# A transformer layer's last product, cut by row blocks and with its weights split beforehand

## The chip, the cores and the metric

One core of one Trainium2 chip. The metric is the device time of one execution in microseconds; a time is the median of several executions. The engines are called PE (matmul), PEld (its weight load), DVE (vector), ACT (scalar activations), POOL (GpSimd) and SP (which issues transfers).

## The reference

One layer: a sliding-window attention mixer, then a gated embedding, then a final norm, for 512 positions of width 2048. The change touches only the last lines:

```python
y = swa_mixer(hn, swa_w_in[j], swa_w_out[j], swa_sinks[j], rel_bias)
x = x + y
emb = p[i] @ ple_proj[i]                                   # 512x256 @ 256x2048
g = jax.nn.sigmoid(rmsnorm(x, ple_norm[i]) @ ple_gate[i])  # 512x2048 @ 2048x2048
x = x + emb * g
...
return rmsnorm(x, final_g)
```

All is float32.

## The kernel before

**Split operands.** A float32 product is made of three matmuls in the fp32r type: each operand is split into a rounded high part and the rest, and `mm3` (L114 to L119) adds high x high (L117), low x high (L118) and high x low (L119). A split is a copy on ACT (`hi`) and a subtraction on DVE (`lo`); for weights it works on pieces of 128 x 1024.

**Seven products.** The product with `ple_gate` is done on half blocks with seven products instead of eight, in the order `ORDER_PLE = (2, 7, 1, 6, 5, 3, 4)`; the last is product 4. Each product `p` has two units `(p, jj)`, `jj` being a half of 512 columns. A unit takes four weight pieces; for each piece it does 12 matmuls of 512 columns into two PSUM banks (two row blocks `tb` of 128 rows). So a unit is 48 matmuls. Behind products 1, 5, 3 and 4 come the `e` matmuls (`embed`), 6 for a row block, with a piece of `ple_proj` (kind "proj").

**Pieces.** `B` (class `Pieces`) loads weight pieces and splits them in order, two pieces ahead of use, into the tags `whi` and `wlo` of three buffers each, so a split waits until PE is done with the piece three places before. Pieces of products 7, 6 and 4 "grow": one tile stays in SBUF and POOL issues a transfer that adds the next weights into it (`_prepare`, L537), once the piece of the product before is split. Of the last product's pieces, the last two are split in halves of 512 columns into the tags `ah` and `al` (L550 to L558).

**Gates.** `gate` takes a unit's banks, subtracts or adds kept partial sums, and `gated` does for one row block and 512 columns: a sigmoid on ACT (L876), times `e` and plus `x` on DVE (L877, L879), and the sum of squares for the final norm (ACT L881, or DVE L883 in the last row block's second column block). Rows 2 and 3 of the four row blocks, columns 0 and 1 of the four column blocks, come from product 4. `finish` makes a row block's norm from the sums (L895 to L904: the root on ACT, the rest on DVE), and `store` scales and writes it (L911 on DVE for rows 0 and 1; L915 and L917 on DVE and ACT for rows 2 and 3, which POOL has multiplied by `final_g` before, L887 and L984 to L986). Rows 2 and 3 issue half their stores from ACT's queue.

**Order.** PE and SP keep the order in which the program is written. In this stage the order of ACT, DVE and POOL is chosen by the framework's scheduler, which takes what is ready by its own reckoning; each engine then works through its queue in that order. In the program's text, `todo` and `later` spread the side work over a unit's four pieces.

**The last product before.** Unit (4,0) runs over both row blocks with its pieces from `B`. Then, for the second column half, row block 0 over 512 columns and row block 1 in two halves of 256 (L987 to L1004), tile `last`, each followed by `embed` and `gated`.

Of the kernel before, what the change touches and what calls it, by code (L numbers as in the profile page):

```python
# [39 lines left out]
PAD = 40  # L40
# [13 lines left out]
def trunk_kernel(ctx: ExitStack, tc: tile.TileContext, a: dict):  # L54
# [88 lines left out]

    def rsqrt_mean(out, ssq, n, nm):
# [12 lines left out]
        nc.vector.tensor_mul(out, y, t)  # L157
# [20 lines left out]
    for k in range(KC):  # L178
# [44 lines left out]
        if k == 9:  # L223
            rsqrt_mean(rstd1, ssq1, D, "r1")
# [298 lines left out]
    class Pieces:  # L523
# [22 lines left out]
        def _split(self, i):  # L546
            raw = self.base.pop(i)
            if i > len(self.specs) - 3:

                self.made[i] = [], []  # L550
                for k in range(2):
                    hi = acts.tile([P, 512], F32R, tag="ah", name=f"bhi{i}_{k}")
                    lo = acts.tile([P, 512], F32R, tag="al", name=f"blo{i}_{k}")
                    nc.scalar.copy(hi, raw[:, k * 512 : (k + 1) * 512])
                    nc.vector.tensor_sub(lo, raw[:, k * 512 : (k + 1) * 512], hi.bitcast(F32))
                    self.made[i][0].append(hi)
                    self.made[i][1].append(lo)
                return  # L558
            hi = wpool.tile([P, WE], F32R, tag="whi", name=f"bhi{i}")
            lo = wpool.tile([P, WE], F32R, tag="wlo", name=f"blo{i}")  # L560
            nc.scalar.copy(hi, raw)  # L561
            nc.vector.tensor_sub(lo, raw, hi.bitcast(F32))  # L562
            self.made[i] = tuple([t[:, :512], t[:, 512:]] for t in (hi, lo))
# [3 lines left out]
        def ahead(self, i):  # L567
            last = len(self.specs) - 1
# [22 lines left out]
    def add_stage(nm, order):  # L591
# [7 lines left out]
        for p in order:  # L599
            for jj in range(2):  # L600
                if (p, jj) == (4, 1):
                    add_embeds(p, jj)
# [9 lines left out]
                if (p, jj) != (4, 1):  # L612
# [134 lines left out]
    def run(gen):  # L747
        for _ in gen:
            pass

# [121 lines left out]
    def gated(t, j, zin, z, e_ps, c=slice(0, 512)):  # L872

        n = done[t]
        done[t] += 1
        nc.scalar.activation(z, zin, AF.Sigmoid, scale=rstd2[:, t : t + 1])  # L876
        nc.vector.tensor_mul(z, e_ps[:, c], z)  # L877
        xt = x1[j][:, t, c]
        nc.vector.tensor_add(xt, xt, z)  # L879
        if (t, j) != (3, 1):  # L880
# [5 lines left out]
        if (t, j) in ((2, 1), (3, 1)):  # L886
            nc.gpsimd.tensor_mul(xt, xt, fg[:, j * 512 + c.start : j * 512 + c.stop])  # L887

    def finish(t):

        n = done[t]
        base, ms, rt, y, nw, yn = (
            const.tile([P, 1], F32, name=f"{v}_{t}") for v in ("base", "ms", "rt", "y", "nw", "yn")
        )
        nc.vector.tensor_reduce(base, ssq3[:, t, : n - 1], axis=AX.X, op=ALU.add)  # L895
        nc.vector.tensor_scalar(base, base, 1.0 / D, EPS, op0=ALU.mult, op1=ALU.add)
        nc.vector.scalar_tensor_tensor(
            out=ms, in0=ssq3[:, t, n - 1 : n], scalar=1.0 / D, in1=base, op0=ALU.mult, op1=ALU.add
        )
        nc.scalar.activation(rt, ms, AF.Sqrt)  # L900
        nc.vector.reciprocal(y, rt)
        nc.vector.scalar_tensor_tensor(out=nw, in0=y, scalar=ms, in1=y, op0=ALU.mult, op1=ALU.mult)
        nc.vector.tensor_scalar(nw, nw, -0.5, 1.5, op0=ALU.mult, op1=ALU.add)
        nc.vector.tensor_mul(yn, y, nw)  # L904
        return [partial_of(store, t, j, yn) for j in range(4)]

    def store(t, j, yn):
        xt = x1[j][:, t, :]
        queue = nc.sync
        if t < 2:  # L910
            nc.vector.scalar_tensor_tensor(  # L911
                out=xt, in0=xt, scalar=yn, in1=fg[:, j * 512 : (j + 1) * 512], op0=ALU.mult, op1=ALU.mult
            )
        elif j < 2:
            nc.vector.tensor_scalar_mul(xt, xt, yn)  # L915
        else:
            nc.scalar.mul(xt, xt, yn)  # L917
            queue = nc.scalar
        queue.dma_start(a["out"][t * P : (t + 1) * P, j * 512 : (j + 1) * 512], xt)
# [4 lines left out]
    def gate(p, jj, ps, e):  # L924

        zs = []
        for tb in range(2):
# [13 lines left out]
            elif p == 3:  # L941
                zs.append((tb, 2 + jj, ps[tb], late.tile([P, 512], F32, tag="junk", name=f"z{jj}_{tb}", bufs=3)))
            else:
                nc.vector.tensor_sub(v2, ps[tb], v2)
                zs.append((2 + tb, jj, v2, v2))
        later[:0] = [partial_of(gated, *z, e[z[0]]) for z in zs]

    for n, p in enumerate(ORDER_PLE):
        nxt = ple_forms.steps(ORDER_PLE[n + 1]) if n < 6 else iter(())
        for jj in range(2):  # L950

            def todo():
                if turns:
                    turn(*turns.pop(0), "s")
                    if not turns:
                        nc.vector.tensor_reduce(ss2, ssq2, axis=AX.X, op=ALU.add)
                        rsqrt_mean(rstd2, ss2, D, "r2")
# [5 lines left out]
            if (p, jj) == (4, 1):  # L963
                break
            ps = unit(p, jj, at_ple, ple_forms, todo)
            e = {}
            if p in (1, 5, 3, 4):
# [3 lines left out]
            later.insert(0, partial_of(gate, p, jj, ps, e))  # L971
        run(nxt)
        if p == 3:
            for t in range(2):
                later.append(partial_of(lambda t: later.extend(finish(t)), t))


    f = ple_forms.made[4]
    first = at_ple[4, 1]
    w = B.get(first - 1)  # L980
    last = [B.get(first + m) for m in range(4)]
    for j in (2, 3):
        for t in (2, 3):
            later.append(partial_of(nc.gpsimd.tensor_mul, x1[j][:, t, :], x1[j][:, t, :], fg[:, j * 512 : (j + 1) * 512]))  # L984
    for t in (2, 3):
        later.append(partial_of(nc.gpsimd.tensor_mul, x1[0][:, t, :], x1[0][:, t, :], fg[:, :512]))  # L986
    for tb in range(2):  # L987
        cuts = [slice(0, 512)] if tb == 0 else [slice(0, 256), slice(256, 512)]
        for n, c in enumerate(cuts):
            ps = bank(f"last{tb}_{n}", "ps"[n])  # L990
            for k in range(8):
                fh, fl = f[k // 2]
                bh, bl = last[k // 2]
                mm3(ps[:, c], fh[:, k % 2, blk(tb)], fl[:, k % 2, blk(tb)], bh[k % 2][:, c], bl[k % 2][:, c], k == 0, k == 7)
                if tb == 0 and k % 2:
                    some_later(4 - k // 2)
            while later:
                later.pop(0)()
            e_ps = embed(2 + tb, w, "o", c)
            z = s2[:, 1, tb, c]  # L1000
            nc.vector.tensor_sub(z, ps[:, c], z)
            gated(2 + tb, 1, z, z, e_ps, c)
        for part in finish(2 + tb):
            part()  # L1004
# [47 lines left out]
```

## Time and profile before

| | us |
|---|---|
| median of 3 runs | 811.64 (811.55 to 811.79) |
| the profiled execution, its own time | 812.79 |
| its span in the profile | 811.1 |
| PE busy in the span | 797.9 |
| DVE busy | 586.4 |
| ACT busy | 469.0 |
| granted TensorE clock, mean of the span | 0.994 |

The profile is of one execution. Each engine row gives busy time, share and number of instructions; a line such as L562 is a line of the kernel. Timeline rows give the start, the duration, the engine and line, the operation, the tile written and those read, and in brackets the idle time before it with what ended it. The duration of a pipelined instruction is longer than the step to the next one, so costs in a row of instructions are taken start to start.

### The profile page before, as it was taken

How to read it: one execution, taken by the hardware profiler on the slowest of the kernel's cores; microseconds unless marked ns; L12 is line 12 of the kernel's file. 1: busy time of each engine (PE TensorE's matmuls, PEld its weight loads, DVE VectorE, ACT ScalarE, POOL GpSimd, SP SyncE). 2: the span in 40 equal slices, each digit the busy share in tenths (PEclk: the TensorE clock that was granted, in tenths of full speed). 3: DMA queues.
4: the chain of work that ended last, by engine and by line, in shares of the span. 5: the costliest groups of instructions: out<-in, count | busy, mean ns of one | idle time of the engine just before them, and what ended most of it. 6: DMA issues, size and time to landing. Idle time of an engine off the chain costs nothing.

```text
span 811.1 us, 11205 instructions
## 1 busy us (share of the span) xinstructions
PE 797.9 (98%) x3924; PEld 670.5 (83%) x3924; DVE 586.4 (72%) x971; ACT 469.0 (58%) x909; POOL 123.6 (15%) x225
## 2 busy tenths in 40 slices
PE   9999999999999999999999999999999999999985
PEld 8888888888888888888888888888888888888874
DVE  4537677777777777776787797766656977779794
ACT  5635455575555565554565754555578756556754
POOL 0102113122121313112121100020000120203012
PEclk9999999999999999999999999999999999999998
DMA  8752688777787967877785369997503995976423
GB/s 331 282 193 90 161 271 200 225 198 208 204 209 208 229 193 188 229 215 192 213 177 133 104 235 341 349 266 242 202 27 130 347 216 199 180 204 201 132 91 118
DMA packets 45145, 164.92 MB, mean 203 GB/s; under 512 B 5904, under 2 KB 8080, under 8 KB 41248
## 3 DMA queue, kind: packets, MB, share of 16 engines
q1 hardware_dynamic: 37792, 129.54, 47.1%
q0 software_dynamic: 6720, 33.61, 22.1%
q10 hardware_dynamic: 576, 1.05, 0.4%
q8 instruction: 31, 0.51, 0.2%
q14 instruction: 26, 0.21, 0.1%
HBM read 158.36 MB, written 46.19 MB: 252 GB/s over the span
## 4 chain that ended last, share of the span: by engine, by line
PE 93%; DVE 2%; issue 2%; ACT 1%; DMA 1%; POOL 1%; SPq 0%; POOLq 0%; ACTq 0%
PE qps L117 7%; PE qps L119 7%; PE qps L118 7%; PE gps L117 7%; PE gps L119 7%; PE gps L118 7%; PE o L119 6%; PE o L117 6%; PE o L118 6%; PE g L118 6%; PE g L119 6%; PE g L117 6%; PE s L367 3%; PE o L446 2%; PE pt L410 2%
## 5 line engine op out<-in xcount | busy, mean ns | idle before, releaser
L562 DVE TENSOR_TENSOR blo<-braw,bhi 128x1024 fp32r<-128x1024 f32 x80 | 98.5, 1232 | 38.4 <-ACT bhi L561 38.3
L561 ACT CAST bhi<-braw 128x1024 fp32r<-128x1024 f32 x80 | 84.1, 1051 | 58.2 <-PE g L119 17.7
L117 PE MATMUL gps<-xh,whi 128*128 128x512 f32 x256 | 100.6, 393 | 0.0
L119 PE MATMUL gps<-xh,wlo 128*128 128x512 f32 x256 | 99.9, 390 | 0.0
L118 PE MATMUL gps<-xl,whi 128*128 128x512 f32 x256 | 99.9, 390 | 0.0
L398 ACT ACTIVATE t<-t,sm 128x129 f32<-128x129 f32 x128 | 50.7, 397 | 70.1 <-DVE sm L395 70.0
L117 PE MATMUL qps<-xh,whi 128*128 128x512 f32 x224 | 88.2, 394 | 0.0
L117 PE MATMUL o<-bhi,fho 128*128 128x512 f32 x224 | 87.7, 391 | 0.0
L119 PE MATMUL qps<-xh,wlo 128*128 128x512 f32 x224 | 87.5, 391 | 0.0
L118 PE MATMUL qps<-xl,whi 128*128 128x512 f32 x224 | 87.3, 390 | 0.0
L104 DVE TENSOR_TENSOR wlo<-wraw,whi 128x1024 fp32r<-128x1024 f32 x60 | 73.3, 1222 | 19.2 <-ACT whi L103 16.4
L119 PE MATMUL o<-bhi,flo 128*128 128x512 f32 x224 | 87.2, 389 | 0.0
L118 PE MATMUL o<-blo,fho 128*128 128x512 f32 x224 | 87.2, 389 | 0.0
L117 PE MATMUL g<-bhi,fhg 128*128 128x512 f32 x208 | 81.3, 391 | 0.0
L119 PE MATMUL g<-bhi,flg 128*128 128x512 f32 x208 | 81.0, 389 | 0.0
L118 PE MATMUL g<-blo,fhg 128*128 128x512 f32 x208 | 80.9, 389 | 0.0
L422 POOL TENSOR_SCALAR_AFFINE_SELECT own<-r 64x512 fp32r<-64x512 f32 (+1 forms) x48 | 33.3, 694 | 300.6 <-DVE r L413 300.6
L103 ACT CAST whi<-wraw 128x1024 fp32r<-128x1024 f32 x60 | 62.7, 1044 | 17.5 <-PE gps L118 9.8
L562 DVE TENSOR_TENSOR blo<-grown,bhi 128x1024 fp32r<-128x1024 f32 x38 | 46.5, 1223 | 21.7 <-ACT bhi L561 21.7
L119 PEld LDWEIGHTS gps<-xh,wlo 128*128 128x128 f32 x256 | 48.1, 188 | 10.4
L117 PEld LDWEIGHTS gps<-xh,whi 128*128 128x128 f32 x256 | 48.2, 188 | 8.8
L118 PEld LDWEIGHTS gps<-xl,whi 128*128 128x128 f32 x256 | 48.2, 188 | 8.6
(193 smaller groups left out, 1685.0 us busy)
## 6 DMA issues: line engine op xcount, KB each, us to landing
wraw<-in_w_gate_in SPq DMA_DIRECT2D x32, 512.0 KB, 5.4
wraw<-in_w_q SPq DMA_DIRECT2D x28, 512.0 KB, 4.9
w_out<-in_w_out POOLq DMA_DIRECT2D x24, 512.0 KB, 7.8
braw<-in_w_out SPq DMA_DIRECT2D x24, 512.0 KB, 3.3
braw<-in_ple_gate SPq DMA_DIRECT2D x24, 512.0 KB, 4.2
w_out<-in_w_out SPq DMA_DIRECT2D x16, 512.0 KB, 6.4
ple_gate<-in_ple_gate SPq DMA_DIRECT2D x16, 512.0 KB, 5.8
ple_gate<-in_ple_gate POOLq DMA_DIRECT2D x16, 512.0 KB, 7.4
```

Source lines behind the costliest of these rows:

```text
L103: nc.scalar.copy(hi, raw)
L104: nc.vector.tensor_sub(lo, raw, hi.bitcast(F32))
L117: nc.tensor.matmul(ps, sh, mh, start=first, stop=False, skip_group_check=more)
L118: nc.tensor.matmul(ps, sh, ml, start=False, stop=False, skip_group_check=more)
L119: nc.tensor.matmul(ps, sl, mh, start=False, stop=last, skip_group_check=more)
L367: nc.tensor.matmul(s_ps[:, u * 192 : u * 192 + 192], st, key[:, low, (g - 2) * HB : (g + 1) * HB], start=low == 0, stop=low == 1,)
L398: nc.scalar.activation(su, su, AF.Exp, bias=sm[:, u : u + 1], accum_out=sm[:, 2 + u : 3 + u])
L410: nc.tensor.transpose(pt[:, u * P : (u + 1) * P], pr[:, u, :], ident)
L422: nc.gpsimd.affine_select(out=flat(own), in_=flat(r).bitcast(F32), pattern=[[0, 8], [sign, HB]], compare_op=ALU.is_ge, fill=0.0, base=-HB ...
L446: nc.tensor.matmul(out, first, r[:, low], start=low == 0, stop=own is None and low == 1)
L561: nc.scalar.copy(hi, raw)
L562: nc.vector.tensor_sub(lo, raw, hi.bitcast(F32))
```

## The change

The last product leaves the loop over units. It becomes four blocks, named `(jj, tb)` as in the code's call (column half, row block), in the order (0,0) and (1,0), which complete row block 2, then (0,1) and (1,1), which complete row block 3. Each block runs over all eight steps of the inner dimension and then its `e`; the last is in two halves of 256 columns. From the end of unit (3,1) on, all five engines keep the written order. Seven of the product's eight pieces are split one by one at written places in the units (5,0), (5,1), (3,0) and (3,1), the eighth behind them, into rooms of their own: a new tile `spare`, quarters whose data is used up, and the room of the piece split before. The two `e` pieces come in front of the eight. The products with `final_g` go from POOL to DVE. The last norm takes its root straight from the last sum of squares, with the rest as a bias. Only the last row block stores two tiles from ACT's queue. `PAD` grows by 64 elements; the kernel also allots fewer one-column tiles in the same pool.

```diff
-PAD = 40
+PAD = 104
...
         nc.scalar.activation(rt, ms, AF.Sqrt)
+        yield
         nc.vector.reciprocal(y, rt)
...
         def _split(self, i):
             raw = self.base.pop(i)
-            if i > len(self.specs) - 3:
...
+        def split_last(self, k, hi, lo):
+            i = len(self.specs) - 8 + k
+            raw = self.base.pop(i)
+            nc.scalar.copy(hi, raw)
+            nc.vector.tensor_sub(lo, raw, hi.bitcast(F32))
+            self.made[i] = tuple([t[:, :512], t[:, 512:]] for t in (hi, lo))
...
-            last = len(self.specs) - 1
+            last = len(self.specs) - 9
...
-                if (p, jj) == (4, 1):
-                    add_embeds(p, jj)
+                if nm == "ple_gate" and (p, jj) == (4, 0):
+                    for v in range(2):
+                        at["e", v] = len(B.specs)
+                        add_embeds(p, v)
...
         nc.scalar.activation(z, zin, AF.Sigmoid, scale=rstd2[:, t : t + 1])
+        yield
         nc.vector.tensor_mul(z, e_ps[:, c], z)
...
         nc.vector.tensor_add(xt, xt, z)
+        yield
...
-        if (t, j) in ((2, 1), (3, 1)):
-            nc.gpsimd.tensor_mul(xt, xt, fg[:, j * 512 + c.start : j * 512 + c.stop])
-    def finish(t):
...
+    def by_gain(t, j):
+        nc.vector.tensor_mul(x1[j][:, t, :], x1[j][:, t, :], gain(j))
+    def store(t, j, queue=nc.sync):
+        queue.dma_start(a["out"][t * P : (t + 1) * P, j * 512 : (j + 1) * 512], x1[j][:, t, :])
+    def row(t, j, yn):
+        xt = x1[j][:, t, :]
+        nc.vector.scalar_tensor_tensor(out=xt, in0=xt, scalar=yn, in1=gain(j), op0=ALU.mult, op1=ALU.mult)
...
+    spare = late.tile([P, 2 * WE], F32R, name="spare")
+    rooms4 = {}
+    early = {(5, 0, 3): 0, (5, 1, 2): 1, (5, 1, 3): 2, (3, 0, 1): 3, (3, 0, 3): 4, (3, 1, 0): 5, (3, 1, 2): 6}
+    def split_last(k):
+        if k == 0:
+            B.split_last(k, spare[:, :WE], spare[:, WE:])
+            return
+        if k % 2:
+            rooms4[(k - 1) // 2] = quarter(f"last{k}").rearrange("p k t -> p (k t)").bitcast(F32R)
+        lo = late.tile([P, WE], F32R, tag="grown", name=f"low{k}", bufs=8)
+        B.split_last(k, rooms4[(k - 1) // 2][:, (k - 1) % 2 * WE : ((k - 1) % 2 + 1) * WE], lo)
+    for n, p in enumerate(ORDER_PLE[:-1]):
...
             def todo():
+                k = early.get((p, jj, next(calls)))
...
+                if k is not None:
+                    split_last(k)
...
+    ctx.enter_context(
+        tc.manual_schedule(
+            engines={getattr(mybir.EngineType, v) for v in ("PE", "SP", "DVE", "Activation", "Pool")}
+        )
+    )
+    w = [B.get(at_ple["e", jj]) for jj in range(2)]
     f = ple_forms.made[4]
+    def block(jj, tb, tag, e_tag, c=slice(0, 512)):
+        ps = bank(f"last{jj}_{tb}_{c.start}", tag)
+        for k in range(8):
+            fh, fl = f[k // 2]
+            bh, bl = B.made[at_ple[4, jj] + k // 2]
+            mm3(ps[:, c], fh[:, k % 2, blk(tb)], fl[:, k % 2, blk(tb)], bh[k % 2][:, c], bl[k % 2][:, c], k == 0, k == 7)
+        e_ps = embed(2 + tb, w[jj], e_tag, c)
+        z = s2[:, jj, tb, c]
+        def opened():
+            nc.vector.tensor_sub(z, ps[:, c], z)
+            return gated(2 + tb, jj, z, z, e_ps, c)
+        return opened
+    two = gate(3, 1, ps, e)
+    for g in two:
+        next(g)
+    for g in two:
+        next(g)
+    split_last(7)
+    for g in two:
+        run(g)
...
+    nc.vector.tensor_reduce(ssum[:, :2], ssq3[:, :2, :4], axis=AX.X, op=ALU.add)
+    root = rsqrt_mean(yn2[:, :2], ssum[:, :2], D, "r3")
+    next(root)
+    g = block(0, 0, "s", "o")()
+    run(root)
+    next(g)
+    for j in range(4):
+        row(0, j, yn2[:, 0:1])
+        store(0, j)
+    next(g)
+    run(g)
+    for j in range(4):
+        row(1, j, yn2[:, 1:2])
+        store(1, j)
+    g = block(1, 0, "s", "t")()
+    next(g)
     for j in (2, 3):
+        by_gain(2, j)
+    next(g)
+    run(g)
+    for j in (2, 3):
+        by_gain(3, j)
+    nc.vector.tensor_reduce(ssum[:, 2:], ssq3[:, 2, :4], axis=AX.X, op=ALU.add)
+    root = rsqrt_mean(yn2[:, 2:], ssum[:, 2:], D, "r4")
+    next(root)
+    g = block(0, 1, "p", "o")()
+    run(root)
+    next(g)
+    for j in range(2):
+        row(2, j, yn2[:, 2:])
+        store(2, j)
+    for j in (2, 3):
+        nc.scalar.mul(x1[j][:, 2, :], x1[j][:, 2, :], yn2[:, 2:])
+        store(2, j)
+    next(g)
+    run(g)
...
+    g = block(1, 1, "p", "t", slice(0, 256))()
+    next(g)
+    by_gain(3, 0)
+    next(g)
+    last = block(1, 1, "s", "o", slice(256, 512))()
+    next(last)
+    run(g)
...
+    nc.vector.tensor_reduce(base, ssq3[:, 3, : n - 1], axis=AX.X, op=ALU.add)
+    nc.vector.tensor_scalar(base, base, 1.0 / D, EPS, op0=ALU.mult, op1=ALU.add)
+    next(last)
+    run(last)
+    lastsq = ssq3[:, 3, n - 1 : n]
+    nc.scalar.activation(rt, lastsq, AF.Sqrt, scale=1.0 / D, bias=base)
+    nc.vector.scalar_tensor_tensor(out=ms, in0=lastsq, scalar=1.0 / D, in1=base, op0=ALU.mult, op1=ALU.add)
+    nc.vector.reciprocal(im, ms)
+    nc.vector.scalar_tensor_tensor(out=nw, in0=rt, scalar=im, in1=rt, op0=ALU.mult, op1=ALU.mult)
+    nc.vector.tensor_scalar(nw, nw, -0.5, 1.5, op0=ALU.mult, op1=ALU.add)
+    nc.vector.scalar_tensor_tensor(out=yn, in0=rt, scalar=im, in1=nw, op0=ALU.mult, op1=ALU.mult)
+    for j, h in ((0, 2), (1, 3)):
+        if j:
+            row(3, j, yn)
+        else:
+            nc.vector.tensor_scalar_mul(x1[j][:, 3, :], x1[j][:, 3, :], yn)
+        nc.scalar.mul(x1[h][:, 3, :], x1[h][:, 3, :], yn)
+        store(3, j)
+        store(3, h, nc.scalar)
```

More of the change, by code (lines that the diff above doesn't have):

```diff
@@ L142, in trunk_kernel, with run @@
     ssq1 = const.tile([P, NB], F32, name="ssq1")
+    def run(gen):
+        for _ in gen:
+            pass
     def rsqrt_mean(out, ssq, n, nm):
@@ L885, in gated, with gain @@
             )
-        if (t, j) in ((2, 1), (3, 1)):
-            nc.gpsimd.tensor_mul(xt, xt, fg[:, j * 512 + c.start : j * 512 + c.stop])
-    def finish(t):
[L891 to L907, printed above, removed]
-        xt = x1[j][:, t, :]
[L909 to L919, printed above, removed]
+    def gain(j):
+        return fg[:, j * 512 : (j + 1) * 512]
+    def by_gain(t, j):
[3 more added lines that the diff above has]
+    def row(t, j, yn):
+        xt = x1[j][:, t, :]
+        nc.vector.scalar_tensor_tensor(out=xt, in0=xt, scalar=yn, in1=gain(j), op0=ALU.mult, op1=ALU.mult)
     s2, s7 = partial("s2"), partial("s7")
@@ L970, in trunk_kernel @@
                     e[t] = embed(t, w, "to"[jj])
-            later.insert(0, partial_of(gate, p, jj, ps, e))
+            if (p, jj) != (3, 1):
+                later.insert(0, partial_of(gate_later, p, jj, ps, e))
         run(nxt)
-        if p == 3:
-            for t in range(2):
-                later.append(partial_of(lambda t: later.extend(finish(t)), t))
-    f = ple_forms.made[4]
-    first = at_ple[4, 1]
-    w = B.get(first - 1)
-    last = [B.get(first + m) for m in range(4)]
-    for j in (2, 3):
-        for t in (2, 3):
-            later.append(partial_of(nc.gpsimd.tensor_mul, x1[j][:, t, :], x1[j][:, t, :], fg[:, j * 512 : (j + 1) * 512]))
@@ L985, in trunk_kernel @@
[L985 to L1004, printed above, removed]
+    while later:
+        later.pop(0)()
```

41 lines of the change are left out of this document (15 added, 26 removed).

## The prediction

> **What bounds the kernel now.** I read the page first, for the span and its bound; then the chain of waits, for the place where something other than TensorE sets the end; then the queues of PE, DVE and ACT at that place.
>
> ```profile
> span 811.1 us, 11205 instructions
> PE 797.9 (98%) x3924; PEld 670.5 (83%) x3924; DVE 586.4 (72%) x971; ACT 469.0 (58%) x909; POOL 123.6 (15%) x225
> PE 93%; DVE 2%; issue 2%; ACT 1%; DMA 1%; POOL 1%; SPq 0%; POOLq 0%; ACTq 0%
> ```
>
> PE is busy for 98% and is 93% of the chain: matmul time can fall only by matmuls not done or by gaps. So I look for gaps. From 600 us on the table of PE's waits has one row:
>
> ```profile
> PE last L118 <- DVE blo L562: 2.0, 1, 2.0
> ```
>
> The last product waits for the low part of a weight piece. PE's timeline around it:
>
> ```profile
> 769.27 0.39 PE L117 MATMUL g<-bhi,fhg 128*128 128x512 f32 x1
> 780.15 0.39 PE L117 MATMUL e<-bhi,pTh 128*128 128x512 f32 x1
> 782.87 0.39 PE L117 MATMUL last<-bhi,fhg 128*128 128x512 f32 x1
> 783.41 0.50 PE L118 MATMUL last<-blo,fhg 128*128 128x512 f32 x1
> 784.67 0.39 PE L117 MATMUL last<-bhi,fhg 128*128 128x512 f32 x1
> 787.07 0.50 PE L118 MATMUL last<-blo,fhg 128*128 128x512 f32 x1 [2.01 <-DVE blo L562]
> 788.10 0.61 PE L119 MATMUL last<-bhi,flg 128*128 128x512 f32 x1
> 791.49 0.41 PE L118 MATMUL last<-blo,fhg 128*128 128x512 f32 x1
> 794.05 0.28 PE L117 MATMUL last<-bhi,fhg 128*128 128x256 f32 x1
> 801.12 0.28 PE L119 MATMUL e<-bhi,pTl 128*128 128x256 f32 x1
> ```
>
> From 769.27 to 780.15 unit (4,0) starts 48 matmuls: 10.88 / 48 = 0.2267 us each, the undisturbed pace at 512 columns. The 12 of its `e` end the unit at 782.87. From 794.05 to 801.12 are 59 steps at 256 columns: 7.07 / 59 = 0.120 us. Between 784.67 and 787.07 stand 2.40 us where 0.23 belong, and behind the stall the eight steps from 788.10 to 791.49 take 3.39 us, 0.42 each: half the pace. So the stall costs twice, 2.2 us of waiting and 3.39 - 8 x 0.2267 = 1.6 us of slow matmuls.
>
> Busy time by stretches shows the same (columns: stretch, its length, busy time and count of PE, PEld, DVE, ACT and POOL, granted clock, DMA share, GB/s):
>
> ```profile
> 728.47:742.07 13.60, 13.60 (x61) 11.26 (x60) 13.48 (x15) 9.98 (x15) 3.52 (x2) 1.00 0.59 192
> 782.87:796.47 13.60, 11.45 (x52) 9.02 (x51) 10.59 (x16) 5.03 (x10) 3.86 (x2) 0.87 0.24 91
> 714.87:769.27 54.40, 54.40 (x241) 45.05 (x240) 43.76 (x53) 34.67 (x49) 6.48 (x4) 1.00 0.55 181
> ```
>
> 1.00 through the units in front, 0.87 in the stretch with the stall. [...]
>
> Why the piece is late is in DVE's queue:
>
> ```profile
> 784.54 0.68 DVE L877 TENSOR_TENSOR s<-e,s 128x512 f32<-128x512 f32 x1
> 785.14 0.74 DVE L911 SCALAR_TENSOR_TENSOR x<-x,yn,fg 128x512 f32<-128x512 f32 x1
> 785.80 1.22 DVE L562 TENSOR_TENSOR blo<-grown,bhi 128x1024 fp32r<-128x1024 f32 x1
> 786.93 0.68 DVE L879 TENSOR_TENSOR x<-x,s 128x512 f32<-128x512 f32 x1
> ```
>
> The split stands behind gate and output work of other rows. Start to start this gives DVE's prices: 785.14 - 784.54 = 0.60 us for a 512-wide two-input op, 0.66 for the one with the gain, 1.13 for a split.
>
> **The change, part by part.** *Matmuls.* The old part is 48 + 12 + 24 + 6 at 512 and 60 at 256; the new one three blocks of 24 + 6 at 512 (90) and 60 at 256. The work is equal, only its order differs. With all pieces ready it starts at 769.27 and lasts 90 x 0.2267 + 60 x 0.120 = 27.60 us, to 796.87; now the last matmul starts at 801.12 and its step ends at 801.24. **Gain 4.37 us**: the wait, the slow stretch, and 0.6 in small steps such as 782.87 to 783.41.
>
> *Seven splits move ahead.* Units (5,0) to (3,1) are 714.87 to 769.27: DVE 43.76 of 54.40 us busy, ACT 34.67. By groups of lines, they hold of the last product's pieces already:
>
> ```profile
> L555 DVE TENSOR_TENSOR blo<-grown,bhi 128x512 fp32r<-128x512 f32 x4 | 2.8, 693 | 1.5 <-ACT bhi L554 1.5
> L562 DVE TENSOR_TENSOR blo<-grown,bhi 128x1024 fp32r<-128x1024 f32 x2 | 2.4, 1222 | 0.3 <-ACT bhi L561 0.3
> ```
>
> Four halves and two whole ones are four splits. Now come seven, and the two `e` pieces that today follow behind 769: five more, 5 x 1.13 = 5.7 us on DVE, 5 x 1.05 on ACT. That is 49.4 and 39.9 of 54.40. POOL's products leave these units (`by_gain` runs on DVE, behind 769), and with them the DVE ops that are slow beside POOL:
>
> ```profile
> 730.90 1.46 POOL L756 TENSOR_TENSOR x<-x,fg 128x512 f32<-128x512 f32 x1 [20.24 <-ACT s L881]
> 731.11 1.79 DVE L879 TENSOR_TENSOR x<-x,s 128x512 f32<-128x512 f32 x1
> 734.57 1.79 DVE L656 TENSOR_TENSOR flg<-hT,fhg 128x512 fp32r<-128x512 f32 x1
> 745.04 1.05 ACT L561 CAST bhi<-braw 128x1024 fp32r<-128x1024 f32 x1 [1.67 <-PE g L119]
> 746.12 1.23 DVE L562 TENSOR_TENSOR blo<-braw,bhi 128x1024 fp32r<-128x1024 f32 x1 [0.21 <-ACT bhi L561]
> ```
>
> The tightest unit is (5,1): 13.48 of 13.60 us of DVE, plus two splits (2.26), less 2 x (1.79 - 0.68) = 2.22: still just full, with (3,0) behind it emptier. The cover is the lead of a split: unit (3,0) starts at 742.07 and a piece lasts 12 x 0.2267 = 2.72, so the split that ends at 747.35 is for the piece that PE begins at 742.07 + 3 x 2.72 = 750.23: 2.9 us early. Cost: zero while DVE is less than 2.9 us late; beyond that each late piece costs a stall, by the rows above 2.0 + 1.6 = 3.6. I take zero, with one stall as the upper end. A gain is excluded, since PE doesn't wait there (54.40 of 54.40).
>
> *The pieces themselves* must have landed. The additions into the last product's pieces are issued by POOL, the last one here, with the landing times of that line below it:
>
> ```profile
> 709.81 0.85 POOL L537 DMA_DIRECT2D grown<-in_ple_gate  x1 [2.16 <-PE g L119]
> ```
>
> ```profile
> DMA to landing us min/median/max: 5.1/6.7/13.0
> ```
>
> With the longest landing the last piece is there at 722.8, and `early` asks for piece 0 in step 3 of (5,0), at 714.87 + 4 x 2.72 = 725.8. Nothing is waited for, in written order.
>
> *DVE in written order behind 769.* It now also does POOL's products. The first product with `e` needs six of the twelve `e` matmuls in front of 769.27: 769.27 - 6 x 0.2267 = 767.9, about 768.1 with the end of the last one. From there to the last half's subtraction I count 18 ops at 0.60 (10 of the gates, 3 subtractions, 5 of `by_gain`), 10 with gain at 0.66, one split at 1.13, 14 one-column ops at about 0.2 and three 256-wide ones at 0.44: 22.6 us, where 28.2 are there. Between the subtractions of (0,0) and (1,0) it is 0.6 + 1.0 + 8 x 0.66 + 1.2 = 8.1 against PE's 6.8, so DVE falls 1.3 us behind; up to the next subtraction it needs 4.6 of 6.8 and has caught up. PE isn't held by this: each block's bank was emptied a block or more before. Cost 0; bounds 0 to 3 us. Square roots among the sigmoids take five table loads behind 769, as many as now; the four in front lie in ACT's waits for a block.
>
> *The tail.* The chain and the queue at the end now:
>
> ```profile
> 800.50 0.95 ACTq L919 DMA_DIRECT2D out<-x  x2
> 800.72 0.42 DVE L1001 TENSOR_TENSOR s<-last,s 128x256 f32<-128x256 f32 x1
> 801.50 0.52 ACT s L876
> 803.62 0.20 ACT L900 ACTIVATE rt<-ms 128x1 f32<-128x1 f32 x1 [0.31 <-DVE ms L897]
> 804.06 0.22 DVE L902 SCALAR_TENSOR_TENSOR nw<-y,ms 128x1 f32<-128x1 f32 x1
> 804.69 0.88 DVE L915 TENSOR_SCALAR x<-x,yn 128x512 f32<-128x512 f32 x2
> 805.32 0.71 ACT x L917
> ```
>
> ```profile
> out<-x ACTq DMA_DIRECT2D x4, 256.0 KB, 3.5
> ```
>
> Subtraction to the first scaled row is 3.97 us. After: subtraction 0.42; sigmoid at 0.44, not at 0.78 (I take the two stores that ACT issues from 800.50 on for what held it, and it issues none there any more), done at 0.95. From the sigmoid's start to the root's is 2.12 us now; the one-column op in front of the root goes (0.19, the root reads the square itself), but the square and sums of the first half now stand on DVE in front of the product and hold it for about as long: 2.12. From the root to the first scaled row is 1.07 now; its last steps become one op shorter, but begin behind a reciprocal that runs beside the root: 1.08, as the op at 804.06 takes 0.25 to the next. That is 0.44 + 2.12 + 1.08 = 3.64, **0.33 us less**. If the sigmoid starts no sooner, 0; the four stores behind it stay, two on SP and two on ACT, so the 5.1 us from ACT's last product (806.03) to 811.1 stay. Two stores of row 2 move from ACT's queue to SP's: behind them wait only the last row's, 4 us later. Cost 0.
>
> In the tail the table load is 1.28 us and the root could follow it at once. [...]
>
> ```profile
> 798.05 1.28 ACT L876 ACT_TABLE_LOAD   x1
> 799.35 0.51 ACT L876 ACTIVATE s<-s,rstd 128x256 f32<-128x256 f32 x1
> ```
>
> *Sum*, against the profiled execution: span 811.1 - 4.37 - 0.33 = 806.4; its own time was 812.79, so 808.1. The median of the three runs, 811.64, lies 1.15 below that one: **806.9**.
>
> **The rivals.** *Slower: the early splits come in front of splits that PE needs at once.* In units (5,0) to (3,0) ACT and DVE aren't in written order, so an early split can land in front of a just-in-time one, or wait there for its landing (up to 722.8). For it: (5,1) has no DVE time left. Against: five splits more in 54.40 us, of which DVE has 10.6 idle. It decides once two pieces come over 2.9 us later than now: two stalls with their slow stretches, 7.2 us, give 806.9 + 7.2 = 814.1. Chance 0.16.
>
> *One such stall*: 806.9 + 3.6 = 810.5, within what can't be told from no change: measurement tells about 0.2%, 1.6 us. 0.06. *The change doesn't do what it says*: the early splits end late all the same and the last product stalls as now, 811.6. 0.02.
>
> *DVE's written order becomes the bound of the end*: the 1.3 us of block (1,0) aren't made good and grow by as much in a second block: 1.3 to 2.6 us of the gain are lost, about 809. For it: 8.1 against 6.8. Against: 5.6 us of room in all. 0.08.
>
> *The slow stretch is not the stall's.* If the half pace from 788.10 on came from something else that stays, 1.6 us of the gain would stay out: 808.5. Against: the clock was 1.00 in all stretches in front. 0.02. [...]
>
> *The load takes twice its time*: the root could start at 0.95 + 2 x 1.28 = 3.5 instead of 2.56, 0.9 us later, 807.8. Against: 1.30 from load to sigmoid. 0.01. [...]
>
> **How the numbers follow.** The forecast has the remaining 0.65. Faster by over 0.2%: 0.65 + 0.08 + 0.02 + 0.01 = 0.76; within: 0.06 + 0.02 = 0.08; slower: 0.16. The range ends above at no change, 811.6, which takes in the one stall; below at 805.5, where the end behind ACT's last product takes 3.7 us and not 5.1 (a store of ACT's lands in 3.5 by its row). Beyond it lie the slower case and 0.04 more. The forecast's own range is 805.5 to 808.
>
> **What would show it.** PE's waits from 600 us on: no row for the last product. The clock 1.00 in every stretch of 13.6 us up to 796. The block's first matmul at about 769.3 and the last `e` at about 796.8; the last half's subtraction at 796.4 and the first scaled row at 800.0. Five table loads from 770 on; no POOL product. Wrong would be a wait of PE on a `blo` or `bhi` before 769, a clock below 1.00 in a unit of products 5 or 3, or DVE still at work when the last half's matmuls end.

## The result and the profile after

| | before | after |
|---|---|---|
| median, us | 812.33 (811.26 to 813.36, 9 executions) | 808.98 (808.38 to 810.51, 9 executions) |
| profiled execution, its own time, us | 812.79 | 808.84 |
| its span, us | 811.1 | 807.0 |
| mean granted clock in it | 0.994 | 0.997 |

The ratio is 0.996 (95% interval 0.995 to 0.9971): 3.35 us less, where 4.7 were forecast from three executions of the kernel before. The forecast time was 806.9 us, with 805.5 to 808 as its own range; 808.98 lies above that range and inside the wide one, which ends at no change (811.6). The page of the changed kernel, the lines that answer to those of before:

```profile
span 807.0 us, 11172 instructions
PE 796.2 (99%) x3924; PEld 669.8 (83%) x3924; DVE 585.1 (72%) x967; ACT 467.8 (58%) x906; POOL 110.2 (14%) x216
PE 85%; issue 8%; DMA 2%; DVE 2%; POOL 2%; ACT 1%; SPq 0%; ACTq 0%; POOLq 0%; DVEq 0%
```

PE's busy time fell only from 797.9 to 796.2; the other 2.4 us of the span were idle time. PE's share of the chain fell from 93% to 85%, because the chain leaves PE at a late split near 713 us, shown below, and runs through other engines and their waits back to 630 us. The table of waits from 590 us on has no row for PE any more. Its weight loads (PEld) have one, and it isn't in the last product:

```profile
PEld g L118 <- DVE blo L556: 0.5, 1, 0.5
```

PE's timeline at that wait, which lies in unit (6,1), and at both ends of the last product:

```profile
712.49 0.39 PE L117 MATMUL g<-bhi,fhg 128*128 128x512 f32 x1
712.92 0.50 PE L118 MATMUL g<-blo,fhg 128*128 128x512 f32 x1
713.26 0.39 PE L119 MATMUL g<-bhi,flg 128*128 128x512 f32 x1
...
769.95 0.39 PE L117 MATMUL last<-spare,fhg 128*128 128x512 f32 x1
...
797.42 0.28 PE L119 MATMUL e<-bhi,pTl 128*128 128x256 f32 x1
```

From 769.95 to the end of the last step, 797.42 + 0.12, are 27.59 us; before, 769.27 to 801.24 were 31.97. At 712.49 two steps take 0.43 and 0.34 us where 0.23 each belong: 0.3 us lost. The stretches of 13.6 us around units (6,1), (5,1) and the end (columns as in the prediction):

```profile
701.27:714.87 13.60, 13.55 (x60) 10.88 (x59) 12.38 (x14) 9.71 (x12) 3.40 (x4) 1.00 0.92 158
728.47:742.07 13.60, 13.60 (x61) 11.27 (x60) 12.43 (x15) 11.39 (x17) 0.00 (x0) 1.00 0.52 170
782.87:796.47 13.60, 13.60 (x86) 12.31 (x85) 11.45 (x25) 7.29 (x12) 0.00 (x0) 1.00 0.45 153
```

The last one had PE busy 11.45 us at a clock of 0.87 before; now 13.60 at 1.00. In unit (5,1) POOL is gone and DVE has more room than before (12.43 against 13.48), although it does more splits.

Where the early splits ran is read from ACT's timeline (their copies are L563), which also shows the tail:

```profile
696.28 1.05 ACT L563 CAST spare<-grown 128x1024 fp32r<-128x1024 f32 x1 [1.53 <-DMA grown<-in_ple_gate]
...
701.92 1.06 ACT L563 CAST last<-grown 128x1024 fp32r<-128x1024 f32 x1 [0.52 <-DMA grown<-in_ple_gate]
...
708.30 1.05 ACT L563 CAST last<-grown 128x1024 fp32r<-128x1024 f32 x1 [1.11 <-DMA grown<-in_ple_gate]
...
797.48 0.51 ACT L878 ACTIVATE s<-s,rstd 128x256 f32<-128x256 f32 x1 [2.82 <-DVE s L998]
798.01 1.28 ACT L1066 ACT_TABLE_LOAD   x1
799.49 0.29 ACT L1066 ACTIVATE rt<-ssq,base 128x1 f32<-128x1 f32 x1 [0.19 <-DVE s L886]
...
801.83 0.72 ACT L1077 ACTIVATE x<-x,yn 128x512 f32<-128x512 f32 x1 [0.45 <-ACT x L1077]
```

With two more at 699.42 and 705.18, five of the seven early copies stand between 696 and 709, in product 6. The code writes the first of them into (5,0), which begins near 715. In the units of product 6 ACT and DVE are ordered by the scheduler, and it moved them up. Four of the five waited for their transfer (all but the one at 699.42). DVE's timeline:

```profile
710.51 1.22 DVE L564 TENSOR_TENSOR low<-grown,last 128x1024 fp32r<-128x1024 f32 x1
711.65 1.22 DVE L556 TENSOR_TENSOR blo<-grown,bhi 128x1024 fp32r<-128x1024 f32 x1
...
731.79 0.69 DVE L881 TENSOR_TENSOR x<-x,s 128x512 f32<-128x512 f32 x1
...
783.82 0.69 DVE L998 TENSOR_TENSOR s<-last,s 128x512 f32<-128x512 f32 x1
...
789.19 0.69 DVE L998 TENSOR_TENSOR s<-last,s 128x512 f32<-128x512 f32 x1 [0.70 <-PE last L119]
...
797.02 0.42 DVE L998 TENSOR_TENSOR s<-last,s 128x256 f32<-128x256 f32 x1 [1.25 <-PE last L119]
...
800.66 0.49 DVE L1076 TENSOR_SCALAR x<-x,yn 128x512 f32<-128x512 f32 x1
```

An early split (L564, 710.51) stands directly ahead of the regular one (L556, 711.65) for which PE waits at 712.49. So the wait in (6,1) is the mechanism of the "slower" rival, one product further forward and at a small part of its price.

### The profile page after: what moved, and what is told of

It reads as the page before. It is cut to its first block, busy times and chain, and to the rows that moved or that the text cites. A ratio compares the mean times of both kernels' runs of the same rounds, so it can differ in the third digit from the quotient of the medians.

```text
span 807.0 us, 11172 instructions
## 1 busy us (share of the span) xinstructions
PE 796.2 (99%) x3924; PEld 669.8 (83%) x3924; DVE 585.1 (72%) x967; ACT 467.8 (58%) x906; POOL 110.2 (14%) x216
## 4 chain that ended last, share of the span: by engine, by line
PE 85%; issue 8%; DMA 2%; DVE 2%; POOL 2%; ACT 1%; SPq 0%; ACTq 0%; POOLq 0%; DVEq 0%
PE qps L117 7%; PE qps L119 7%; PE qps L118 7%; PE gps L117 7%; PE gps L119 7%; PE gps L118 7%; PE o L119 6%; PE o L117 6%; PE o L118 6%; PE s L372 3%; PE g L118 2%; PE g L119 2%; PE g L117 2%; PE o L451 2%; PE pt L415 2%
## 5 line engine op out<-in xcount | busy, mean ns | idle before, releaser
L556 DVE TENSOR_TENSOR blo<-braw,bhi 128x1024 fp32r<-128x1024 f32 x80 | 97.8, 1223 | 41.6 <-ACT bhi L555 41.6
L117 PE MATMUL g<-bhi,fhg 128*128 128x512 f32 x192 | 75.1, 391 | 0.0
L118 PE MATMUL g<-blo,fhg 128*128 128x512 f32 x192 | 74.9, 390 | 0.0
L119 PE MATMUL g<-bhi,flg 128*128 128x512 f32 x192 | 74.9, 390 | 0.0
L556 DVE TENSOR_TENSOR blo<-grown,bhi 128x1024 fp32r<-128x1024 f32 x32 | 39.1, 1223 | 17.4 <-ACT bhi L555 17.4
```

Of the source, the lines that this page charges most:

```text
L117: nc.tensor.matmul(ps, sh, mh, start=first, stop=False, skip_group_check=more)
L118: nc.tensor.matmul(ps, sh, ml, start=False, stop=False, skip_group_check=more)
L119: nc.tensor.matmul(ps, sl, mh, start=False, stop=last, skip_group_check=more)
```

## The experiments

The theory after the result: the gain is the removed stall and tail as forecast; it came out 1.35 us smaller because (a) the slow stretch behind the stall isn't in every execution of the kernel before, and (b) the early splits cost something in (6,1). Rivals: DVE or the end of the program became the bound, or something else in the change carries the gain. Times on one chip are compared with the same executions of the kernel before there; the changed kernel itself ran in two sets, 808.98 and 808.84 us.

**The early splits held at their written places.** Each is made to follow the newest regular split in the order of ACT and DVE:

```diff
-            nc.scalar.copy(hi, raw)
-            nc.vector.tensor_sub(lo, raw, hi.bitcast(F32))
+            with tc.issue_after(self.newest[0]), tc.issue_after(self.newest[1]):
+                nc.scalar.copy(hi, raw)
+                nc.vector.tensor_sub(lo, raw, hi.bitcast(F32))
```

> The changed kernel with one thing more: each early split is queued behind the weight split written last before it, so it can't move forward into product 6. Theory A (five early splits ran at 696 to 711 in front of splits that PE needed, waited there for their transfers and cost PE 0.4 us at 712.9): no step of PE over 0.25 us between 700 and 715, the early splits at 724 to 766, DVE fuller there but no wait of PE, the last product starting 0.3 to 0.5 us sooner counted from the turn of x at 596; time 0.4 to 1.0 us under the changed kernel's 809.0, so 808.0 to 808.6. Rival B (the missing 1.4 us come from somewhere else, or from a different spread of the runs): within 0.3 us of the changed kernel. Rival C (the written places are too tight for DVE, 13.7 of 13.6 us in unit (5,1)): a wait of PE on a split at 740 to 752, time 1 to 4 us above the changed kernel.

808.60 us (807.83 to 809.02), ratio 0.9957 (0.9944 to 0.9969), span 806.4. ACT's and PE's timelines:

```profile
724.21 1.05 ACT L565 CAST spare<-grown 128x1024 fp32r<-128x1024 f32 x1
...
735.58 1.05 ACT L565 CAST last<-grown 128x1024 fp32r<-128x1024 f32 x1
```

```profile
712.18 0.39 PE L117 MATMUL g<-bhi,fhg 128*128 128x512 f32 x1
712.40 0.39 PE L118 MATMUL g<-blo,fhg 128*128 128x512 f32 x1
...
769.30 0.39 PE L117 MATMUL last<-spare,fhg 128*128 128x512 f32 x1
```

The splits stand in (5,0) and later, the step at 712 is 0.22 us, and the last product starts at 769.30, as early as the prediction had it. DVE in (5,1) was not too full for them: PE has no wait there. In the trace the lost step is gone, and PE's share of the chain is 95%; in time the two kernels' executions overlap (0.4 us between medians, in different sets of runs).

**Both last products of ACT ahead of both of its stores.**

```diff
         nc.scalar.mul(x1[h][:, 3, :], x1[h][:, 3, :], yn)
         store(3, j)
-        store(3, h, nc.scalar)
+    for h in (2, 3):
+        store(3, h, nc.scalar)
```

> The changed kernel with ACT's two last products in front of its two last stores. Theory (in the written order the second product waits for the first one's store to be issued): the second product starts 0.65 us behind the first instead of 1.17, the last store is issued 0.5 us sooner, and the time falls by 0.3 to 0.5 us. Rival (the end is set by the rate at which the four last stores, 1.05 MB, move): the second product is sooner but the time changes by less than 0.15 us.

808.72 us (808.46 to 809.45), ratio 0.9961 (0.9949 to 0.9974), span 806.7. ACT's timeline:

```profile
800.48 1.33 ACT L1077 ACTIVATE x<-x,yn 128x512 f32<-128x512 f32 x2 [0.87 <-DVE yn L1071]
801.23 0.95 ACTq L897 DMA_DIRECT2D out<-x  x2
```

The second product no longer waits 0.45 us for the issue of a store, but the end comes 806.7 - 800.48 = 6.22 us behind the first product, against 807.0 - 800.66 = 6.34: 0.1 gained, less than the 0.3 to 0.5 expected, as the rival had it. What follows the last product sets the end, not that product; whether it is the rate of the stores was not tested.

**The stall back.** Split 7 is written behind the first output row of row block 1, so that PE waits for it about as long as in the kernel before:

```diff
-    split_last(7)
...
     for j in range(4):
+        if j == 1:
+            split_last(7)
         row(1, j, yn2[:, 1:2])
         store(1, j)
```

> The changed kernel with the split of piece 7 written behind the first output row of row block 1 (same work, other place), so that it ends near 783.0 while PE wants the piece at 780.8. Theory A (the old stall cost its wait and a slow stretch of about 3.4 us behind it): a wait of about 2.1 us in block (1,0), then some eight steps at 0.43 us, the block's end 3.7 us later and the time 3.3 to 3.8 us above the changed kernel. Rival B (a wait of 2 us costs itself only, the slow stretch had another cause): wait of 2.1 us, all later steps at 0.227, time 1.8 to 2.2 us above the changed kernel.

813.81 us (812.12 to 814.97, 10 executions), ratio 1.0022 (1.0013 to 1.0031). PE's timeline:

```profile
783.60 0.50 PE L117 MATMUL last<-last,fhg 128*128 128x512 f32 x1 [2.00 <-ACT last L563]
784.86 0.51 PE L118 MATMUL last<-low,fhg 128*128 128x512 f32 x1 [0.76 <-DVE low L564]
785.21 0.39 PE L119 MATMUL last<-last,flg 128*128 128x512 f32 x1
785.43 0.39 PE L117 MATMUL last<-last,fhg 128*128 128x512 f32 x1
```

The edit made two waits, not one, because ACT's copy came late as well. And behind them the steps are 0.22 us: in the profiled execution, of mean clock 0.996, there is no slow stretch at all. The ten executions fall into two groups: three of mean clock 0.996 or 0.997 at 812.12 to 813.25, seven of 0.992 to 0.994 at 813.46 to 814.97, so neither theory holds for all of them. The stretch seems to follow a stall in some executions only, so the clock is to be read for every execution of the kernel before. Half the clock for 3.4 us of 811 (granted 0.50 from 788.10 to 791.49 in the profile of before) lowers the mean by 0.002, which is the step between the groups:

| the kernel before, its four sets together | executions | median, us | from, to |
|---|---|---|---|
| mean clock 0.994 or 0.995 | 27 | 812.76 | 811.95 to 813.91 |
| mean clock 0.996 or 0.997 | 31 | 811.43 | 810.77 to 812.63 |

The two are 1.3 us apart, near the 1.6 us that the slow steps lost in the profile of before, whose own clock was 0.994. Only one execution of a set has a trace, so the others' waits are not shown; had those without the stretch also waited less, the groups would lie more than 1.6 us apart. A single value of 0.995 proves little: one execution of the changed kernel (808.84) and one of the version with held splits (807.83) have it too, without such a wait.

**A short and a long wait.** The question is whether the stretch depends on how long PE waits. Only the low part of piece 7 is moved, in front of row block 1's output rows, or behind all four of them:

```diff
-    split_last(7)
+    low7 = split_last(7)
...
     for j in range(4):
+        if j == 0:
+            low7()
         row(1, j, yn2[:, 1:2])
         store(1, j)
```

The second kernel has `low7()` behind this loop instead.

> The changed kernel; only the low part of piece 7 is written later, in front of the output rows of row block 1, so that PE waits for it once. [...] Rival (any wait halves the pace behind it in four runs of ten): some runs at 0.994 and 1.5 us longer.

> The same with the low part of piece 7 behind all four output rows of row block 1. Theory: a wait of about 4.0 us, a slow stretch of some eight steps at 0.43 us behind it in all or nearly all runs (clock 0.994 or less), time 4.0 + 1.6 = 5.6 us above the changed kernel, 814.6. Rival (a slow stretch in four runs of ten whatever the wait): most runs at 0.996, median 4.0 us above.

The changed kernel ran once more on the chip of these two:

> The changed kernel once more, on the chip on which the next three run, so that they are compared with it there. Theory: every run at a mean clock of 0.996 or more, since nothing in it waits long enough for a slow stretch; runs of the kernel before of the same call fall into two groups, about 811.3 us at clock 0.996 and 812.7 at 0.994. Rival (the clock groups are chance and have nothing to do with the wait): a third or more of its runs at 0.994 too.

The changed kernel took 808.84 us (808.61 to 809.22), ratio 0.9959 (0.9947 to 0.9972), four of five executions at a clock of 0.996 or 0.997 and one at 0.995. The short wait took 810.62 (809.97 to 811.31, 11 executions), ratio 0.9977 (0.9968 to 0.9986), all at a clock of 0.996 or 0.997. The long one took 814.71 (814.22 to 816.26, 6 executions), ratio 1.0035 (1.0022 to 1.0047), all at 0.992 to 0.994. PE's timeline with the short wait, then with the long one:

```profile
781.55 0.39 PE L117 MATMUL last<-last,fhg 128*128 128x512 f32 x1
783.16 0.50 PE L118 MATMUL last<-low,fhg 128*128 128x512 f32 x1 [1.22 <-DVE low L1030]
783.50 0.39 PE L119 MATMUL last<-last,flg 128*128 128x512 f32 x1
783.73 0.39 PE L117 MATMUL last<-last,fhg 128*128 128x512 f32 x1
```

```profile
780.72 0.39 PE L117 MATMUL last<-last,fhg 128*128 128x512 f32 x1
784.98 0.79 PE L118 MATMUL last<-low,fhg 128*128 128x512 f32 x1 [3.87 <-DVE low L1031]
785.58 0.63 PE L119 MATMUL last<-last,flg 128*128 128x512 f32 x1
786.00 0.63 PE L117 MATMUL last<-last,fhg 128*128 128x512 f32 x1
```

Behind 1.4 us lost in the wait the steps are 0.23 us, behind 4.0 us they are 0.42. Against the changed kernel of the same chip the long wait costs 5.9 us by the medians and 5.4 in its profiled execution (814.22): 4.0 of waiting and 1.5 of slow steps, seven from 784.98 to 788.04. The short one costs 1.8: 1.4 in the wait, 0.1 in the step behind it, and 0.2 in unit (6,1), where its profile has a step of 0.66 and the changed kernel's on that chip 0.50. Counted by mean clock, the slow stretch came more often the longer the wait: never at 1.4 us (0 of 11), in about half of the executions at 2.2 us (27 of 58, the kernel before), always at 4.0 us (6 of 6).

**The tail's claim by itself**, on the kernel before: row 2's stores leave ACT's queue.

```diff
-            queue = nc.scalar
+            queue = nc.scalar if t == 3 else nc.sync
```

> The kernel before with one thing changed: row block 2's two stores of ACT's queue go to SP's. Theory A (the last half's sigmoid was held from 0.44 to 0.78 us behind its subtraction by those two store issues): the sigmoid starts 0.44 to 0.5 us behind the subtraction and the time falls by 0.3 us (0.1 to 0.4). Rival B (it waited for DVE's square of the first half, as the releaser in the profile says): sigmoid at 0.78 as before, no change within 0.15 us.

811.75 us (810.89 to 812.94, 11 executions), ratio 0.9999 (0.999 to 1.0008): not resolved in time. Its wait in the last product is that of the kernel before (2.0 us by its row), and 6 of its 11 executions have a clock of 0.994 or 0.995. DVE's and ACT's timelines, then ACT's row of the kernel before:

```profile
800.90 0.42 DVE L1001 TENSOR_TENSOR s<-last,s 128x256 f32<-128x256 f32 x1
...
804.62 0.88 DVE L915 TENSOR_SCALAR x<-x,yn 128x512 f32<-128x512 f32 x2
```

```profile
801.36 0.51 ACT L876 ACTIVATE s<-s,rstd 128x256 f32<-128x256 f32 x1
```

```profile
801.50 0.51 ACT L876 ACTIVATE s<-s,rstd 128x256 f32<-128x256 f32 x1 [0.42 <-DVE s L883]
```

The sigmoid starts 0.46 us behind the subtraction, not 0.78, and the first scaled row 3.72 behind it, not 3.97. ACT's own store issues had held the sigmoid, although the row of before names DVE's sum of squares of the first half (L883) as what it waited for. Here that sum ends at 801.66, after the sigmoid has begun, so it is not what held it.

**The pin and the order of the tail together**, same chip as the changed kernel's second set.

> The two edits that the first runs spoke for, together in the changed kernel: early splits pinned behind the split written before them, and ACT's two last products in front of its two last stores. Theory: 0.4 us from the pinned splits (PE's lost steps at 712) and 0.2 us from the tail, so 0.4 to 0.8 us under the changed kernel of this call. Rival (what the pinned splits give doesn't reach the time): within 0.2 us of it.

808.34 us (808.06 to 808.56), ratio 0.9952 (0.994 to 0.9965), span 806.5: the fastest version. Its slowest execution is under the changed kernel's fastest on that chip (808.61), 0.5 us between medians.

**No written early places.** The table `early` is emptied and pieces 0 to 6 are written behind unit (3,1):

```diff
-    early = {(5, 0, 3): 0, (5, 1, 2): 1, (5, 1, 3): 2, (3, 0, 1): 3, (3, 0, 3): 4, (3, 1, 0): 5, (3, 1, 2): 6}
+    early = {}
...
+    for k in range(7):
+        split_last(k)
     split_last(7)
```

> The changed kernel without its early splits: pieces 0 to 6 are split behind unit (3,1), in written order in front of its gates. Theory A (splitting ahead is what takes the wait off PE; DVE has 5.6 us to spare behind 769 and no 8): PE waits 0.5 to 1 us for piece 0 and 2 to 3 us in front of the first e of block (0,0), whose bank the late gates hold; DVE runs 4 to 6 us late to the end; time 4 to 6 us above the changed kernel, 813 to 815, above the kernel before. Rival B (the blocks and the written order alone bring the gain, as a split of 1.13 us is shorter than the 1.36 us in which PE uses a piece): within 1.5 us of the changed kernel.

808.64 us (808.07 to 809.44), ratio 0.9962 (0.995 to 0.9975): no slower. ACT's timeline says why:

```profile
695.88 1.05 ACT L563 CAST spare<-grown 128x1024 fp32r<-128x1024 f32 x1 [1.82 <-DMA grown<-in_ple_gate]
...
707.95 1.06 ACT L563 CAST last<-grown 128x1024 fp32r<-128x1024 f32 x1 [1.14 <-DMA grown<-in_ple_gate]
```

Written behind unit (3,1), up to 70 us later, five of the splits ran in product 6 all the same. The edit did not do what it was meant to; what it shows is that the written places do not decide when these splits run. So it was repeated with the pin of the first experiment, which holds pieces 0 to 6 behind the last regular split:

> What the run without early splits was meant to be, as that one's schedule kept them early: pieces 0 to 6 are split behind unit (3,1) and each is queued behind the split of the second e piece, so that none can move forward. Theory A (splitting ahead is what the gain needs): PE waits 0.5 to 1 us for piece 0 and 2 to 3 us before the first e of block (0,0), DVE runs 4 to 6 us late to the end, time 4 to 6 us above the changed kernel's 808.9, 813 to 815. Rival B (blocks in rooms of their own are enough, wherever the splits stand): within 1.5 us of the changed kernel.

814.73 us (814.3 to 815.14, 7 executions), ratio 1.0033 (1.0021 to 1.0044). PE's waits, PE's timeline and DVE's:

```profile
PE e L117 <- DVE z L882: 3.0, 1, 3.0
PE last L118 <- DVE spare L566: 0.6, 1, 0.6
```

```profile
779.05 0.50 PE L117 MATMUL e<-bhi,pTh 128*128 128x512 f32 x1 [2.96 <-DVE z L882]
...
780.12 0.63 PE L118 MATMUL e<-blo,pTh 128*128 128x512 f32 x1
780.55 0.63 PE L119 MATMUL e<-bhi,pTl 128*128 128x512 f32 x1
```

```profile
770.59 7.81 DVE L566 TENSOR_TENSOR low<-grown,last 128x1024 fp32r<-128x1024 f32 x6
```

Six splits in a row hold DVE for 7.8 us, the gate behind them doesn't free its bank, and PE waits for that bank and runs slow behind the wait: eight steps at 0.42, from 780.12 to 783.50. The version with the same pin and the early places had 808.60 us on this chip (ratio 0.9957); without the early places it is 6.1 us more. So the blocks and their rooms do not bring the gain when the splits come late in one row; the early places carry it. The 6.1 us are not the price of four pieces ahead against seven: the kernel before had four ahead and this version has none, and late splits spread between the gates were not run.

**Two other parts undone**, each by itself: the products with `final_g` back on POOL, and only PE and SP in written order behind (3,1).

```diff
-        nc.vector.tensor_mul(x1[j][:, t, :], x1[j][:, t, :], gain(j))
+        nc.gpsimd.tensor_mul(x1[j][:, t, :], x1[j][:, t, :], gain(j))
```

> The changed kernel with its five products by the gain on POOL again, at their written places. Theory A (they hide on either engine; POOL's cost is that DVE's ops beside it are slower, 1.8 us instead of 0.7 as in the kernel before): DVE's ops beside them take up to 1.1 us longer, the blocks' slack of about 1.3 us takes most of it, time 0 to 0.6 us above the changed kernel. Rival B (taking 3.0 us off DVE shortens the end): 0.2 us or more under it.

```diff
-            engines={getattr(mybir.EngineType, v) for v in ("PE", "SP", "DVE", "Activation", "Pool")}
+            engines={getattr(mybir.EngineType, v) for v in ("PE", "SP")}
```

> The changed kernel with only PE and SP in written order behind unit (3,1); the order of DVE, ACT and POOL is the scheduler's there as before. Theory A (the gain is the pieces split ahead and the blocks; the written order of the side engines carries only the tail's 0.3 us): no wait of PE in the last product, time within 0.6 us of the changed kernel. Rival B (the written order is what keeps splits in front of gates): PE waits in the last product as in the kernel before, time 2 us or more above the changed kernel.

809.02 us (808.53 to 809.66), ratio 0.9965 (0.9951 to 0.9979), and 808.61 (807.91 to 809.0), ratio 0.996 (0.9947 to 0.9972). Neither differs from the changed kernel, which ran in other sets, by more than its executions scatter; in both, PE's only wait from 590 us on is the one in (6,1). POOL did not run its five products at their written places: it had nothing in front of them and ran four from 731.96 to 752.96, when their data was there. A DVE op beside the first of them took 1.78 us again (732.17). Neither the move to DVE nor the written order of the side engines is needed for the gain.

## Why the prediction was right, and where it was short

**Right.** The last product takes 27.59 us, 27.60 forecast, with no wait and the clock at 1.00. Leaving out POOL brought the DVE op beside it from 1.79 to 0.69 us (731.79). DVE is late for block (1,0) (783.82) and has caught up at the next block's subtraction, where it waits 0.70 us for PE (789.19), and at the last one, 1.25 us (797.02). So the rival that DVE becomes the bound of the end, whose price of about 809 us is nearest to the result, has the number by chance and not the mechanism. The tail from the last subtraction to the first scaled row is 800.66 - 797.02 = 3.64, 3.64 forecast, though two of its parts are off by 0.1 each way: 0.46 + 2.01 + 1.17 against 0.44 + 2.12 + 1.08. The root starts 1.48 behind the begin of its table load, 0.19 of it a wait for DVE: the other 1.29 are the load of 1.28 once and not twice.

**Between the two profiles** the span fell by 4.1, not 4.7. The last product starts at 769.95, not 769.27, 0.68 later; of that, 0.33 is there at the transposes of `x` near 596 already (596.02 before, 596.35 after), ahead of the first early split, and 0.35 arises behind it, nearly all in (6,1). The last product is 4.4 us shorter and what follows it 0.4.

**The first step that failed: "The median of the three runs, 811.64, lies 1.15 below that one: 806.9".** Without this step the forecast is 808.1, 0.9 below the result; with it, 2.1. The prediction read the slow stretch, 1.6 us, in one profiled execution and took its loss off a median. Counted by mean clock, the stretch is in 27 of 58 executions. An execution that has none can't gain its removal. The 1.15 us between the profiled execution and the three shown (all below 811.8) was the sign: those three lie where executions without the stretch lie, though their own clocks are not on record. Priced by kind, the forecast is 3.1 us (the wait, the small steps, the tail) against executions without it and 4.7 against those with it. On one chip the kernel before had 811.43 (7 executions) and 813.12 (9); the version with the pin and the new tail order had 808.34: 3.1 and 4.8 us less. The changed kernel there, at 808.84, gained 2.6 and 4.3.

**The second: "Cost: zero" for the early splits, since "nothing is waited for, in written order".** The written order was not kept in these units, as the rival said. The scheduler put five splits into product 6, four of them ahead of their transfers, and a regular split came late behind one: "a wait of PE on a `blo` or `bhi` before 769", which the prediction had named as a sign of being wrong. POOL's additions moved back too, from 709.81 for the last one to this:

```profile
713.16 0.85 POOL L542 DMA_DIRECT2D grown<-in_ple_gate  x1 [3.17 <-DVE blo L556]
```

The price is 0.3 us in the profiled execution; counted the same way, over the late step and the next, it is 0.4 to 0.8 us in the eight other profiles of the changed kernel and its versions without the pin. The rival had the mechanism, but put it where DVE was fullest and at two stalls of 3.6; DVE's idle time in front of (5,0) took most of it up (9.3 of 13.6 us busy there before, 12.4 after). The 0.5 us of the version with the pin, of which the tail's order has 0.1 by its profile, is of the size of this loss. How it divides between the two edits was not resolved.

**The rival that the slow stretch is not the stall's** fell: it comes and goes with the wait's length, in 0 of 11 executions at 1.4 us and in 6 of 6 at 4.0 us. But the forecast's reading, that each such wait has it, did not hold either.

## What to carry to other kernels

When the profiled execution's own time differs from the median, ask which term of your sum is in that execution alone, and price it by how often it comes: the mean clock of every execution, not only of the profiled one, told this at once. A place in the program's text does not place an instruction on an engine that a scheduler orders; rooms of its own let it run early, and an ordering edge keeps it from running too early. Of the parts that were undone one at a time, only splitting ahead moved the time by more than the scatter; the order of the blocks was not undone by itself.

## What the runs showed of the hardware

A wait of 2.2 us can stand in front of a slow stretch of 3.4 us, in some executions and not in others. Counted by a mean clock of 0.995 or less, with the wait that each version's profiled execution shows, it came in 0 of 11 executions at 1.4 us, 33 of 69 at 2.2 us (27 of 58 of the kernel before, 6 of 11 with row 2's stores moved), 7 of 10 at two waits of 2.2 and 1.0 us (2.0 and 0.8 by their rows), 7 of 7 at waits of 0.7 and 3.1 us (0.6 and 3.0), and 6 of 6 at 4.0 us. The stretch lasts 3.4 us: eight steps at 0.42 in the profile of before (788.10 to 791.49, granted clock 0.50) and eight with the wait of 3.0 us (780.12 to 783.50). In both it began about 1 us after PE had resumed, at 787.07 and at 779.05. Behind 4.0 us the first step was slow already, and the slow steps fill 3.1 us (seven, 784.98 to 788.04). What decides in which executions it comes was not shown.

An activation whose row names DVE as what it waited for can have been held by its own queue's store issues: it starts 0.78 us behind the subtraction with two issues in front (0.95 us from 800.50), 0.46 without.
